# Gate stores of a streaming encoder layer issued from the sync queue instead of ScalarE's

## The chip, the cores and the metric

The kernel runs on one core of a Trainium2 chip. The metric is the device time of one execution in microseconds (us), as the median of several runs. Engines are named as in the profile: PE (matmul), PEld (its weight loads), DVE, ACT (ScalarE), POOL (GpSimd) and SP (the sync engine). SP computes nothing here; it issues transfers. "SPq" and "ACTq" are the instruction queues of SP and ACT where they issue transfers.

## The reference

One step of one encoder layer over 2048 prompt rows and 64 sample rows, 1024 channels, all in float32. Cut to what matters:

```python
h = rms_norm(x, norm1_g) * (1 + sc1) + sh1
z = h @ w_in
glu_a, glu_b, q, k, v, g_conv, g_attn = split(z)      # gates: 2 x 1024 columns
u = glu_a * sigmoid(glu_b)
conv_out = conv_module(u)        # causal depthwise conv of 31 taps, LayerNorm, swish, w_conv_out
o = attend(rms_norm(q), rms_norm(k), v)               # own chunk of 64 and the 8 before it
attn_out = o @ w_attn_out
merged = sigmoid(g_conv) * conv_out + sigmoid(g_attn) * attn_out
x = x + gt1 * (merged @ w_o)
h2 = rms_norm(x, norm2_g) * (1 + sc2) + sh2
x = x + gt2 * ((silu(gate) * up) @ w_ffn_out)         # gate, up = split(h2 @ w_ffn_in)
```

## The kernel before

Every float32 operand of a matmul is split into a high and a low part, and a product is three matmuls (high by high, high by low, low by high), so `hh`/`hl` are the two parts of the normalised input, `whi`/`wlo` those of a weight, `ph`/`pl` those of the softmax.

The 2112 rows are worked off in four blocks, `PBLOCKS`, of 576, 512, 512 and 512 rows. The first phase runs through `ORDER`: for each block the columns of `w_in` in eight stages, `q, 0, k, 1, v, 2, 3, g`. Numbered stages are the GLU pairs of the convolution, `g` the gates. Attention, convolution, norms of the next block and the splitting of weights are laid between the projection's matmuls as generators. Stage `g` of the four blocks lies at about 182 to 320, 481 to 612, 764 to 887 and 1029 to 1171 us. Then the mixers are merged over three column blocks, and the feed-forward part follows.

In stage `g` the inner function `part` of `gates` computes one tile of 128 gate columns by up to 512 rows: 24 matmuls into `ps`, a tanh on ACT from `ps` into a temporary tile `t` named "gate", and a store of that tile to the DRAM tensor `g_d`. There are 84 such tiles: 32 of 128x288 in the first block, 44 of 128x512 and 8 of 128x256 in the others. The merge reads `g_d` back much later (`gate_columns`, L1133).

The tile comes from `temp`:

```python
NT, NS = 7, 2
def temp(name, shape=(P, 512)):
    return wk.tile(list(shape), F32, tag="t", name=name, bufs=NT)
```

All temporaries with tag "t" share these seven buffers, among them `ln` (the convolution's norm), `other` (half of an attention output), `r`/`t` (roots of the norms) and the gates. A buffer is handed on when its last reader is done; for a gate the reader is the store.

What sets the order around the change: PE's order is that of the code, fixed by hand up to the end of the first phase. The orders of ACT, DVE, POOL and SP are laid by a scheduler from the dependences, so a transfer stands in its issuing engine's queue at one place among that engine's other instructions. Each engine works its queue in order; one that waits holds what is behind it. Besides the gates, SP's queue carries the loads of weights (L385 the raw ones, L480 the split ones read back, L515 the split ones written), of keys, queries and values (L1464, L1465, L1471, L1473), of the attention's bias (L1517), of the next block's input rows (`x_t` L1146, `x_c` L1159), and the stores of the attention and convolution parts (`o_d` L1495, `c_d` L1363). `x_t` is squared and summed on ACT; from the sums POOL makes the roots `r`, PE transposes them (`pt`), and the next block's norm goes on from there. All transfers, from either queue, share a set of eight completion semaphores in turn, and one that takes a semaphore waits for the landing of the transfer that had it before.

Of the kernel before, what the change touches and what calls it, by code (L numbers as in the profile page):

```python
# [73 lines left out]
def halves(lo, hi):  # L74
    n = hi - lo
    if n <= 512:
        return [(lo, hi)]
    mid = lo + n // 2
    return [(lo, mid), (mid, hi)]


def tile_chunks(lo, hi):

    tiles = token_tiles(lo, hi)
    t, n = tiles[(len(tiles) + 1) // 2 - 1]
    return [(lo, t + n), (t + n, hi)]
# [537 lines left out]
def streaming_layer(ctx: ExitStack, tc: tile.TileContext, I, O):  # L624
    nc = tc.nc
# [24 lines left out]
    g_d = dram.tile([2, KT, P, T], F32, name="g_d")  # L650
# [127 lines left out]
    def temp(name, shape=(P, 512)):  # L778
        return wk.tile(list(shape), F32, tag="t", name=name, bufs=NT)
# [467 lines left out]
    def columns(wh, wl, hh, hl, c0, c1):  # L1247

        nk = len(wh)
        ps = ps_g.tile([P, 512], F32, tag="gp", name="ps")  # L1250
        for k in range(nk):
            mm3(ps[:, : c1 - c0], wh[k], wl[k], hh[k][:, c0:c1], hl[k][:, c0:c1], k == 0, k == nk - 1)
        return ps

    def kts(t, a=0, b=KT):
        return [t[:, k] for k in range(a, b)]
# [132 lines left out]
    def gates(b, free):  # L1389

        o = PBLOCKS[b][0]
        w = PBLOCKS[b][1] - o

        def part(g, ws, c0, c1):
            ps = columns(*ws, kts(hh), kts(hl), c0, c1)
            t = temp("gate")
            stream.after("act", "pe")
            act.activation(t[:, : c1 - c0], ps[:, : c1 - c0], AF.Tanh, scale=0.5)
            nc.scalar.dma_start(g_d[g // 8, g % 8, :, o + c0 : o + c1], t[:, : c1 - c0])

        def pair(g):
            ws = [W.get(("in", 2560 + g * P, h)) for h in range(2)]
            return [[[w[l][:, k, e * P : e * P + P] for w in ws for k in range(4)] for l in range(2)] for e in range(2)]

        n = 16 - SPLIT_G if b + 1 < len(PBLOCKS) else 16
        for g in range(0, n, 2):
            for e, ws in enumerate(pair(g)):
                for c in halves(0, w):
                    part(g + e, ws, *c)
                if e:  # L1410
                    W.done()
                    W.done()
                yield g + e
        rest = [ws for g in range(n, 16, 2) for ws in pair(g)]
        for c0, c1 in ((0, w // 2), (w // 2, w)):
            for i, ws in enumerate(rest):
                part(n + i, ws, c0, c1)
                if c1 == w and i % 2:
                    W.done()
                    W.done()  # L1420
            free["columns"] = c1
# [531 lines left out]
    c0, c1 = tile_chunks(*CBLOCKS[0])  # L1953
# [517 lines left out]
```

## Time and profile before

| | us |
|---|---|
| runs | 2931.04, 2938.12, 2940.68 |
| median | 2938.12 |
| profiled execution | 2935.84 |
| its span | 2934.1 |
| PE busy in the span | 2877.2 |
| ACT busy | 1366.9 |

The times of a span are of one execution; the execution's own time is 1.74 us longer than the span. "Busy" of an engine leaves out the issuing of transfers. The granted TensorE clock was 0.993 of full speed on average. By the windows over stage `g` and what lies between, the engines were busy as follows (window, length, busy us of PE, PEld, DVE, ACT and POOL with counts, granted clock, busy share of the DMA engines, GB/s):

```profile
180.00:320.00 140.00, 128.80 (x921) 124.81 (x919) 99.31 (x204) 78.64 (x176) 25.90 (x23) 0.94 0.90 299
...
480.00:612.00 132.00, 127.20 (x715) 109.03 (x717) 94.78 (x186) 82.27 (x148) 13.36 (x12) 0.99 0.92 285
...
764.00:887.00 123.00, 121.75 (x687) 105.29 (x686) 87.91 (x177) 79.65 (x143) 12.25 (x12) 1.00 0.94 290
...
1029.00:1175.00 146.00, 142.78 (x790) 122.84 (x789) 104.05 (x201) 98.70 (x174) 23.33 (x15) 1.00 0.85 256
```

In a row of waits, the engine named first waits, "<-" names who ended the wait, and the numbers are total us, times, and the longest.

### The profile page before, as it was taken

The numbers are of one execution on the slowest core, as the hardware profiler recorded it, in microseconds if no ns is written. First come the engines' busy times: TensorE is split into PE (matmuls) and PEld (weight loads), VectorE is DVE, ScalarE is ACT, GpSimd is POOL, SyncE is SP. The second block draws the span as 40 slices with busy tenths as digits, with TensorE's granted clock in tenths as the row PEclk, the third lists the DMA queues.
The fourth block names the chain that finished last, engine by engine and source line by source line (L and its number), as shares of the span: only waits on it lengthen the run. The fifth ranks groups of instructions, "written<-read, shape, count | busy, mean of one in ns | idle before, by whom it ended". The sixth has DMA issues, their size and how long they took to land.

```text
span 2934.1 us, 44538 instructions
## 1 busy us (share of the span) xinstructions
PE 2877.2 (98%) x16130; PEld 2578.7 (88%) x16130; DVE 2044.7 (70%) x3621; ACT 1366.9 (47%) x2441; POOL 1170.4 (40%) x742
## 2 busy tenths in 40 slices
PE   8998999999999999999999999999999999999999
PEld 6798878788888888898999998999999999999998
DVE  5995688578867886487777756666666557566666
ACT  4345634661465267464434345444444345444442
POOL 1301310101011102454566452366667742465767
PEclk9998999999999999999999999999999999999999
DMA  8989889988997897884444876232333965333333
GB/s 320 331 299 320 278 284 307 288 282 288 292 309 233 298 272 238 287 311 166 147 144 144 290 253 215 94 125 87 115 123 104 344 223 180 97 101 108 115 107 127
DMA packets 313788, 634.28 MB, mean 216 GB/s; under 512 B 36864, under 2 KB 133664, under 8 KB 313568
## 3 DMA queue, kind: packets, MB, share of 16 engines
q1 hardware_dynamic: 300464, 612.88, 63.3%
q10 hardware_dynamic: 13104, 18.56, 1.8%
q8 instruction: 127, 2.08, 0.3%
q14 instruction: 93, 0.76, 0.1%
HBM read 482.81 MB, written 148.51 MB: 215 GB/s over the span
## 4 chain that ended last, share of the span: by engine, by line
PE 48%; DVE 2%; ACT 1%; issue 0%; POOL 0%; ACTq 0%; DVEq 0%
PE ps L106 29%; PE pd L106 14%; PE pw L106 5%; DVE wlo L106 1%; DVE pw L106 0%; ACT whi L106 0%; DVE ps L106 0%; DVE t L106 0%; DVE sums L106 0%; PE pt L106 0%; DVE acc L106 0%; ACT xn L106 0%; DVE hid L106 0%; ACT hid L106 0%; DVE b L106 0%
## 5 line engine op out<-in xcount | busy, mean ns | idle before, releaser
L106 PE MATMUL ps<-t,whi 128*128 128x384 f32 (+1 forms) x2112 | 502.1, 322 | 2.1 <-ACT u L106 0.8
L106 POOL TENSOR_TENSOR wlo<-wst,whi 128x1024 fp32r<-128x1024 f32 (+1 forms) x159 | 363.2, 2296 | 239.9 <-ACT whi L106 204.8
L106 ACT ACTIVATE whi<-wst 128x1024 fp32r<-128x1024 f32 (+1 forms) x265 | 257.9, 978 | 294.4 <-PE ps L106 126.7
L106 PE MATMUL ps<-b,whi 128*128 128x384 f32 (+1 forms) x1584 | 378.4, 324 | 4.8 <-DVE v L106 2.1
L106 PEld LDWEIGHTS ps<-t,whi 128*128 128x128 f32 x2112 | 367.6, 188 | 9.5 <-ACT u L106 3.0
L106 DVE SCALAR_TENSOR_TENSOR y<-u,wd,y 128x512 f32<-128x512 f32 (+1 forms) x480 | 369.3, 773 | 7.7
L106 PE MATMUL ps<-hh,whi 128*128 128x512 f32 (+2 forms) x992 | 364.2, 367 | 0.0
L106 DVE TENSOR_TENSOR acc<-acc,pd 128x512 f32<-128x512 f32 x482 | 322.3, 685 | 48.6 <-PE pd L106 46.1
L106 PE MATMUL ps<-hh,wlo 128*128 128x512 f32 (+2 forms) x992 | 346.3, 349 | 0.0
L106 PE MATMUL ps<-hl,whi 128*128 128x512 f32 (+2 forms) x992 | 345.9, 349 | 0.0
L106 PE MATMUL ps<-t,wlo 128*128 128x384 f32 (+1 forms) x1056 | 338.2, 321 | 0.0
L106 PE MATMUL pd<-whi,hid 128*128 128x512 f32 x912 | 297.3, 391 | 0.3 <-DVE hid L106 0.3
L106 PEld LDWEIGHTS ps<-b,whi 128*128 128x128 f32 x1584 | 275.6, 188 | 12.9 <-DVE v L106 3.2
L106 ACT ACTIVATE pr<-pr,sm 128x640 f32<-128x640 f32 (+3 forms) x272 | 202.5, 749 | 154.4 <-DVE sm L106 152.3
L106 PE MATMUL ps<-b,wlo 128*128 128x384 f32 (+1 forms) x792 | 255.0, 322 | 0.0
L106 POOL TENSOR_TENSOR r<-t,mhalf 128x8 f32<-128x8 f32 (+4 forms) x54 | 86.3, 1599 | 395.6 <-DVE t L106 385.4
L106 PEld LDWEIGHTS ps<-hh,wlo 128*128 128x128 f32 x992 | 188.0, 189 | 23.1
L106 PEld LDWEIGHTS ps<-hh,whi 128*128 128x128 f32 x992 | 188.6, 190 | 17.3 <-issue 2.5
L106 PEld LDWEIGHTS pd<-whi,hid 128*128 128x128 f32 x912 | 171.1, 188 | 36.3 <-ACT hid L106 0.7
L106 DVE TENSOR_TENSOR wlo<-wst,whi 128x1024 fp32r<-128x1024 f32 (+1 forms) x106 | 134.5, 1276 | 97.6 <-ACT whi L106 96.4
L106 PEld LDWEIGHTS ps<-hl,whi 128*128 128x128 f32 x992 | 188.9, 190 | 14.8 <-issue 1.7
L106 PEld LDWEIGHTS ps<-t,wlo 128*128 128x128 f32 x1056 | 198.1, 188 | 0.8
(235 smaller groups left out, 6274.6 us busy)
## 6 DMA issues: line engine op xcount, KB each, us to landing
whi<-w_din_h SPq DMA_DIRECT2D x72, 512.0 KB, 6.1
wlo<-w_din_l SPq DMA_DIRECT2D x72, 512.0 KB, 6.9
wst<-sum_d SPq DMA_DIRECT2D x131, 256.0 KB, 2.9
wfo<-in_w_ffn_out SPq DMA_DIRECT2D x64, 512.0 KB, 3.9
sum_d<-ws SPq DMA_DIRECT2D x88, 256.0 KB, 2.2
wst<-in_w_ffn_in SPq DMA_DIRECT2D x85, 256.0 KB, 2.9
wst<-in_w_ca SPq DMA_DIRECT2D x35, 512.0 KB, 5.2
wst<-in_w_ffn_in SPq DMA_DIRECT2D x35, 512.0 KB, 4.6
```

The lines of the kernel that those rows point to most:

```text
L106: self.last = f(*args, **kw)
```

## The change

The store of a gate tile is issued by `nc.sync` instead of `nc.scalar`; the code around it stays.

```diff
             t = temp("gate")
             stream.after("act", "pe")
             act.activation(t[:, : c1 - c0], ps[:, : c1 - c0], AF.Tanh, scale=0.5)
-            nc.scalar.dma_start(g_d[g // 8, g % 8, :, o + c0 : o + c1], t[:, : c1 - c0])
+            nc.sync.dma_start(g_d[g // 8, g % 8, :, o + c0 : o + c1], t[:, : c1 - c0])
```

The scheduler places the 84 stores in SP's queue, between its loads, and orders ACT's and DVE's work anew around them; PE's order in the first phase stays. Numbers behind a name tell instances apart.

SP in the first block's gates, where the fourth `x_t` of the next block is loaded, as it stands after the change (`part_l` is a half of an attention part, `kk` keys, `wst` a raw weight):

```order
L1495 DMA o_d_66<-part_l_2924 128x64
L1399 DMA g_d_68<-gate_2953 128x288
L1399 DMA g_d_68<-gate_3010 128x288
L385 DMA wst_3055<-in_w_qkv 128x1024
L515 DMA w_din_4096_1_h_3057<-whi_3017 128x1024
L515 DMA w_din_4096_1_l_3058<-wlo_3018 128x1024
L1517 DMA bias_192<-in_rel_bias 64x576 x2
L1464 DMA kk_1714<-q_d_63 64x2x64
L1465 DMA kk_1714<-k_d_64 64x320
L1464 DMA kk_1714<-q_d_63 64x2x64
L1465 DMA kk_1714<-k_d_64 64x320
L1399 DMA g_d_68<-gate_3079 128x288
```

The three rows of gates are new; all others stood in the same order before, and four rows further down follows the load of `x_t_3092`.

ACT at the same place, from the difference of the two orders (`ph` is half of a softmax, `whi` a weight's high part, `ssq` the sums of squares):

```order
 L106 ACTIVATE gate_3189<-ps_3140 128x288
 L106 ACTIVATE ph_3177<-ptp_3176 128x128
-L1399 DMA g_d_68<-gate_3189 128x288
+L106 ACTIVATE ln_3221<-y_774,lnh_176 128x64
+L106 ACTIVATE x_t_2892,ssq_2902<-x_t_2892 128x1024
 L106 ACTIVATE ph_3177<-ptp_3176 64x64
-L106 ACTIVATE ln_3221<-y_774,lnh_176 128x64
+L106 ACTIVATE x_t_2894,ssq_2902<-x_t_2894 128x1024
+L106 ACTIVATE x_t_2896,ssq_2902<-x_t_2896 128x1024
```

The store leaves ACT, and the squares of three `x_t`, which stood further up before, now follow the tanh of gate_3189.

SP in the last block's gates, from the difference (`cin` are the merge's first inputs, `tg` the gates read back):

```order
 L1471 DMA vv_11756<-v_d_65 128x8x128
+L1141 DMA cin_11850<-c_d_67 128x4x320
 L1141 DMA cin_11852<-c_d_67 128x4x320
 L1141 DMA cin_11851<-o_d_66 128x4x320
+L1399 DMA g_d_68<-gate_11843 128x512
 L1141 DMA cin_11853<-o_d_66 128x4x320
 L1133 DMA tg_11858<-g_d_68 128x320
```

One store comes in ahead of the last `cin` and of `tg`, and one `cin` has moved down to here; queries, keys and bias for the next group of heads follow behind `tg`.

## The prediction

> **What bounds the kernel now.** I read the page's busy times first, then PE's waits, then the two queues that issue transfers, then single stretches of the four gate stages. The page's first lines, the queue of ScalarE's transfers and the chain of waits:
>
> ```profile
> PE 2877.2 (98%) x16130; PEld 2578.7 (88%) x16130; DVE 2044.7 (70%) x3621; ACT 1366.9 (47%) x2441; POOL 1170.4 (40%) x742
> ...
> q10 hardware_dynamic: 13104, 18.56, 1.8%
> ...
> PE 48%; DVE 2%; ACT 1%; issue 0%; POOL 0%; ACTq 0%; DVEq 0%
> ```
>
> PE is busy for 2877.2 of 2934.1 us, so everything but PE together explains 56.9 us. ACT is at 47%, and ACTq, the queue that issues the 84 stores, has 0% of the chain. A change that only relieves ACT can gain next to nothing; what counts is PE's waits:
>
> ```profile
> PE sc L106 <- DVE sm L106: 9.5, 5, 4.0
> PE pt L106 <- DVE kn L106: 8.7, 4, 4.2
> PE pt L106 <- POOL r L106: 7.2, 1, 7.2
> PE sc L106 <- DMA kk<-k_d: 4.1, 3, 2.3
> ...
> PE ps L106 <- DMA wlo<-w_dqkv_l: 1.5, 2, 0.8
> ...
> PE ps L106 <- ACT gate L106: 1.4, 1, 1.4
> ```
>
> Columns are total us, times, longest. Only one short wait is for a gate's tanh, and the store follows the tanh, so nothing of that 1.4 us goes. The gates' own rows, and what the sync queue waits for:
>
> ```profile
> L106 ACT ACTIVATE gate<-ps x84: 364/576/602, 182.3 to 1170.1; 128x512 f32<-128x512 f32 x44, 128x288 f32<-128x288 f32 x32, 128x256 f32<-128x256 f32 x8
> L1399 ACTq DMA_DIRECT2D g_d<-gate x84: 326/326/359, 182.7 to 1170.8; - x84
> ...
> DMA to landing us min/median/max: 1.7/5.3/8.7
> ```
> ```profile
> SPq L1464 <- DMA g_d<-gate: 23.9, 8, 7.6
> ...
> SPq L1465 <- DMA g_d<-gate: 17.4, 6, 4.6
> ```
>
> Two things show here. A store costs its issuer 0.326 us and lands 5.3 us later. And SP already waits for stores that it did not issue: 23.9 + 17.4 us in 14 waits at two lines alone, since the transfers of both queues take their completion semaphores in turn.
>
> **The change part by part.** Removed: 84 issues of 0.326 us on ACT, 27.4 us. ACT has the other 53% of the span free, so I price it at 0; what covers it is PE's own work, and without that cover 27.4 us would be its limit. Added: the same 84 issues on SP, priced per issue by SP's rows below (0.38 to 0.61 us), 32 to 51 us of SP. PE never waits for SP itself, so this too counts only where a load that PE needs comes later. The bytes (18.56 MB) stay. The real cost is that SP is one queue in order: a store placed in it waits for its tanh, and every load behind it waits along. So I went through the 84 places in SP's new order and compared when SP issued the next load before with when the tanh ended.
>
> *Block 0 (180 to 320 us).* SP runs behind ACT here, so 31 of the 32 stores find their tanh done and cost an issue alone. The stretch holds the two longest stalls of all gate stages. Rows of SP's queue, ACT, DVE, POOL and PE (start, length, engine, what, and in brackets the idle time before it and who ended it):
>
> ```profile
> 253.88 0.61 SPq L1464 DMA_DIRECT2D q<-q_d  x1
> 259.10 0.46 SPq L1465 DMA_DIRECT2D kk<-k_d  x1
> ...
> 265.67 0.38 SPq L1495 DMA_DIRECT2D o_d<-part_l  x1
> ...
> 273.06 0.60 SPq L1465 DMA_DIRECT2D kk<-k_d  x1
> ...
> 276.19 0.50 SPq L1146 DMA_DIRECT2D x_t<-in_x_prompt  x1
> ```
> ```profile
> 266.58 0.41 ACT L106 ACTIVATE gate<-ps 128x288 f32<-128x288 f32 x1 [0.71 <-PE ps L106]
> ...
> 272.36 0.41 ACT L106 ACTIVATE gate<-ps 128x288 f32<-128x288 f32 x1
> ...
> 283.41 1.06 ACT L106 ACTIVATE x_t<-x_t 128x1024 f32<-128x1024 f32 x1 [5.05 <-DMA x_t<-in_x_prompt]
> ```
> ```profile
> 275.36 0.29 DVE L106 CUSTOM_DVE_ANT_0 pr<-sc,bias 128x128 f32<-128x128 f32 x1 [3.59 <-DMA bias<-in_rel_bias]
> ```
> ```profile
> 284.84 1.02 POOL L106 TENSOR_TENSOR r<-t,mhalf 128x4 f32<-128x4 f32 x1 [10.10 <-DMA c_d<-part_l]
> ```
> ```profile
> 268.09 0.19 PE L106 MATMUL po<-ph,vv 128*128 128x64 f32 x1
> ...
> 275.72 0.79 PE L106 MATMUL sc<-kk,q 128*128 128x256 f32 x2 [3.96 <-DVE sm L106]
> ...
> 285.92 0.48 PE L106 MATMUL pt<-ident,r 128*128 128x128 f32 x1 [7.24 <-POOL r L106]
> ```
>
> PE waits 3.96 us until 275.72, because the bias load came late, and 7.24 us until 285.92, because the fourth x_t, issued at 276.19, was there only at 283.41 (square, then r, then pt). Both loads are in SP's queue, so the change can move both stalls, and this is where the sign is decided.
> For earlier: the gap between 254.49 and 259.10 is a wait for a landed gate, 4.61 us, which leaves when SP carries the stores itself; and the stores of gate_3137, 3189 and 3247, which ACT had issued before x_t landed, now stand behind that load.
> For later: by the order 24 of the block's stores stand ahead of the fourth x_t, five of them after 249 us (gate_2832 to gate_3079), 5 x 0.4 = 2 us against the 4.61 us; the others went before it partly into SP's own waits. And the tile that a gate is written to comes from a ring of seven, shared with the norm and attention temporaries; it is free when its store has landed. By the order, gate_2953's store goes behind part_l at 265.67, so it is issued near 266.1 and lands near 271.3; gate_3189 takes that tile, and its tanh, at 266.58 before, comes 4.8 us later. Behind it on ACT stand ph, on which PE's po at 268.09 waits, and now also the x_t squares. PE's work between 268.09 and 271.76 (3.7 us) then runs until about 277, past the 275.72 at which bias let it go on: the first 3.96 us of lateness are covered by that wait. Likewise gate_3079's store goes behind kk at 273.06, lands near 279, and gate_3247's tanh, 272.36 before, waits 6.6 us for it; that falls into PE's wait for r. The fourth x_t is issued behind these, by my count between 276 and 279.
> Bounds: −11.2 us (both stalls gone, 3.96 + 7.24) and +10 (x_t 7 us later and 3 us of slower clock after it). I take +2, the middle of x_t's 0 to 3 us plus the uncovered half microsecond of po, because the issue times of SP are nearer to this case than a queue that runs ahead.
>
> The clock's price is in the windows around these stalls (columns: window, length, busy us of PE, PEld, DVE, ACT, POOL, granted clock, DMA share, GB/s):
>
> ```profile
> 270.00:280.00 10.00, 4.72 (x25) 4.13 (x23) 2.29 (x7) 3.99 (x9) 2.34 (x1) 0.70 0.98 318
> 280.00:290.00 10.00, 4.08 (x17) 4.07 (x18) 3.68 (x8) 1.88 (x5) 1.02 (x1) 0.50 1.03 354
> 290.00:300.00 10.00, 10.00 (x74) 9.91 (x73) 5.78 (x23) 5.43 (x13) 0.00 (x0) 0.95 0.82 305
> ```
>
> The clock granted falls to 0.50 behind the stalls and is 0.95 again after 290: a stall that vanishes would bring a little more than its length, one that appears cost a little more. The Trainium skill, "TensorE: Matmul & The Clock Gate", Part 1 (The HAM clock gate), says that the clock goes to half after at least one idle window of about 3.4 us; by that rule the 3 us that I put into block 3 below leave it at full and the sum as it is, 2940.2, and a wait just longer than the window would bring an estimated 1.7 us more (half of 3.4 us at half clock), 2942; the 0.70 and 0.50 behind waits of 3.96 and 7.24 us agree with it. The DMA engines are full there (0.98 and 1.03), so a store that stands behind loads gives its share to them.
>
> *Block 1 (481 to 612).* From the second store on, SP is ahead of the tanh and gets held. In the order x_t 2 and 3, issued at 517.77 before, go behind gate_6018, whose tanh ends at 553.17 + 0.60 = 553.77:
>
> ```profile
> 517.77 0.90 SPq L1146 DMA_DIRECT2D x_t<-in_x_prompt  x2
> ```
> ```profile
> 553.17 0.60 ACT L106 ACTIVATE gate<-ps 128x512 f32<-128x512 f32 x1
> ```
> ```profile
> 536.45 0.90 PE L106 MATMUL sc<-kk,q 128*128 128x320 f32 x3 [2.29 <-DMA kk<-k_d]
> ```
>
> With them 1 MB leaves the traffic ahead of the kk loads, for which PE waits at 536.45. Bounds: −4.1 us (all waits on kk gone) and +3 (three weights as late as the longest weight wait above, 0.8 us, and half a microsecond elsewhere). I take −1, a little under half of the longest such wait: the keys themselves are issued no earlier, only the traffic ahead of them thins. Behind the third and later stores SP is held 1 to 9 us by a tanh; the weights there are loaded further ahead than that, as PE's short waits on weights above let expect, so the +3 stays in the range alone.
>
> *Block 2 (764 to 887).* By the same comparison gate_8802 holds SP by 11 us and four others by 4 to 9 us; what covers it is again the distance at which keys and weights are loaded. Bounds −0.8 (the longest weight wait above gone) and +4 (five such holds at 0.8 us); I take +0.4, one issue ahead of a weight that came just in time.
>
> *Block 3 (1029 to 1171).* One place is uncovered. SP's loads here, the tanh of gate_11843 on ACT, the matmul that needs the keys, and the median landing of such a load:
>
> ```profile
> 1121.13 1.42 SPq L1133 DMA_DIRECT2D tg<-g_d  x2
> 1128.43 0.61 SPq L1464 DMA_DIRECT2D q<-q_d  x1
> ...
> 1130.39 0.63 SPq L1465 DMA_DIRECT2D kk<-k_d  x1
> ```
> ```profile
> 1128.74 0.58 ACT L106 ACTIVATE gate<-ps 128x512 f32<-128x512 f32 x1
> ```
> ```profile
> 1137.88 0.76 PE L106 MATMUL sc<-kk,q 128*128 128x320 f32 x4
> ```
> ```profile
> kk<-k_d SPq DMA_DIRECT2D x48, 256.0 KB, 7.6
> ```
>
> In the new order the store of gate_11843 stands ahead of the last cin load, tg and the keys. SP can issue it only at 1129.32; then one cin and two tg (about 2.1 us by their rows) and only then q, at 1131.8 instead of 1128.43: 3.4 us later, with the traffic of cin and tg now directly before it. The last kk, issued at 1130.39, is there by its median landing of 7.6 us at 1138.0, and PE takes it at 1137.88: nothing to spare. Bounds 0 (the shared engines make up for it) and +6 (the store's 5.3 us more); I take +3, the 3.4 us less some tenths in which the shared engines are not full.
>
> *The rest.* In the first merge, from 1190 us, PE's order differs in a few rows, and gates are read long after they landed: 0, within −1 and +1.
>
> Sum: 0 + 2 − 1 + 0.4 + 3 + 0 = +4.4 us. The profiled execution took 2935.84 us, 1.74 around its span of 2934.1: 2940.2. That execution lies 2.28 us under the median of 2938.12; I put the new median at 2941, between 2940.2 and 2942.5. What a measurement of this kernel can tell from no change is 0.3%, 8.8 us, and so +3 or +4 reads as the same.
>
> **The rivals.** *Slower:* the ring of seven decides. If gate_2953's store lands later than 271.3, by the 8.7 us that the slowest store took instead of 5.3, ACT and with it po, the squares and x_t all shift: 4.8 + 3.4 = 8.2 us against a cover of 3.96, leaving 4.2; with x_t as late (7 us) after it, and +3 in block 3, it is 2948 to 2952. It decides once the fourth x_t lands later than 290. For it speak 0.98 and 1.03 of DMA share; against it that ACT itself idles 5.05 us before x_t's square.
> *Faster:* SP stops waiting for landed gates (41.3 us at two lines), runs 4 to 7 us ahead, x_t and bias land before PE asks. Then 3.96, 7.24 and some 2.3 us on kk go, +3 stays: 2935.84 − 10.5 = about 2925, 2927 as a median. It needs x_t at 269 instead of 276.19; against it stand the 24 issues added ahead of it, and the completion semaphores that SP's transfers still take in turn.
> *Weights late:* the holds of 9 to 11 us behind a tanh in blocks 1 and 2 exceed the spare time in two or three places, 3 to 4 us each, +10 in all, 2950. Against it: PE waits for no weight there by more than 0.8 us now.
> That the change does not do what it says is excluded: its order shows 84 stores on SP and none on ACT.
>
> *Hidden anyway:* the stores share the DMA engines with the loads from either queue, so only the 84 issues change places, 27.4 us on ACT and 32 to 51 on SP, and neither is on PE's path: 2935.84, as a median 2938. For it speaks ACTq's 0% of the chain; against it the order, in which the tanhs come ahead of loads. The Trainium skill, "DMA: Bandwidth & Descriptors", section Issuing engines are not separate DMA queues, states this rule: transfers from several engines run on the same 16 DMA engines, and spreading them only saves issue time on the sequencer. The trace agrees as far as bytes go, by the 0.98 and 1.03; no run here yet shows the rest.
>
> **How the numbers follow.** Forecast (2936 to 2947 as its own range): 0.38. Hidden anyway: 0.20, also within 0.3%. Slower by the ring in block 0: 0.17. Weights late: 0.10. Faster by SP's freed waits: 0.15. So faster 0.15, same 0.58, slower 0.27. The range goes to 2928 on one side, into the faster case, and to 2954 on the other, into both slower ones; about 0.08 and 0.10 are left out.
>
> **What would show it.** ACT without any issue of line 1399; SP's rows for it 84 times at 0.33 to 0.6 us; SP's waits turned from landed gates to ACT's gate in blocks 1 to 3, and about 11 us of them at gate_8802. PE's wait for r at about 286 of 7 to 10 us, for kk at 536 shorter, and a new wait of some 3 us for sc near 1138. ACT's tanh of gate_3189 near 271 with a wait on a store's landing. Wrong it would be if x_t's fourth load is issued before 272 or lands after 290, or if PE waits for weights in blocks 1 and 2.

## The result and the profile after

| | median us | runs | ratio to before, 95% |
|---|---|---|---|
| before | 2931.98 | 7 (2930.45 to 2940.68) | |
| after | 2946.16 | 7 (2944.65 to 2954.21) | 1.0045 [1.0032, 1.0057] |
| after, once more in a later session | 2947.20 | 6 (2942.11 to 2954.22) | 1.0038 [1.0024, 1.0053] |

Each ratio here and below is to the kernel before, run beside it on the same chip (medians of 2934.66 to 2936.88 us in the later sessions). The change made the kernel slower by 0.45%, 13 us by this ratio. The profiled execution took 2946.04 us, its span is 2943.9, 9.8 us more than before. The page's first lines after the change:

```profile
PE 2879.9 (98%) x16130; PEld 2581.5 (88%) x16130; DVE 2040.7 (69%) x3621; ACT 1366.7 (46%) x2441; POOL 1167.6 (40%) x742
...
q1 hardware_dynamic: 312560, 630.19, 64.6%
...
q10 hardware_dynamic: 1008, 1.25, 0.1%
```

The stores' bytes, 17.3 of the 18.56 MB of queue q10, have moved to q1, and PE's busy time grew by 2.7 us only: the other 7.1 us of the longer span are time in which PE waits. The longest of PE's waits after the change but the first, which hardly differs (total us, times, longest):

```profile
PE sc L106 <- DMA kk<-k_d: 9.4, 4, 4.6
PE pt L106 <- POOL r L106: 9.3, 1, 9.3
PE sc L106 <- DVE sm L106: 9.0, 5, 3.9
```

Waits for keys went from 4.1 to 9.4 us. SP's list of waits shows the other side:

```profile
SPq L1399 <- ACT gate L106: 136.3, 39, 7.9
```

Before, SP waited at 14 places of two lines (41.3 us, and 110 us over all lines) for a gate's store to land. That is gone but for 0.8 us; instead it waits 136.3 us, at 39 of the 84 stores, for the tanh. To see where PE falls behind, read the same matmul in both timelines. The first rows are of the kernel after:

```profile
274.80 0.51 PE L106 MATMUL sc<-kk,q 128*128 128x256 f32 x2 [1.41 <-DVE sm L106]
285.80 0.47 PE L106 MATMUL pt<-ident,r 128*128 128x128 f32 x1 [9.31 <-POOL r L106]
...
534.29 0.82 PE L106 MATMUL sc<-kk,q 128*128 128x320 f32 x4 [1.01 <-DMA kk<-k_d]
...
557.14 0.86 PE L106 MATMUL sc<-kk,q 128*128 128x320 f32 x4 [0.71 <-DVE sm L106]
...
610.35 1.43 PE L106 MATMUL sc<-kk,q 128*128 128x320 f32 x4 [4.58 <-DMA kk<-k_d]
...
634.05 0.82 PE L106 MATMUL sc<-kk,q 128*128 128x320 f32 x4 [1.22 <-DMA kk<-k_d]
...
893.47 1.43 PE L106 MATMUL sc<-kk,q 128*128 128x320 f32 x4 [3.92 <-DVE sm L106]
...
1045.19 0.83 PE L106 MATMUL sc<-kk,q 128*128 128x320 f32 x4 [1.48 <-DVE sm L106]
...
1147.35 1.10 PE L106 MATMUL sc<-kk,q 128*128 128x320 f32 x4 [2.60 <-DMA kk<-k_d]
...
1181.26 0.56 PE L106 MATMUL ps<-cin,whi 128*128 128x320 f32 x2 [1.39 <-ACT gate L106]
```

And of the kernel before, the counterparts of the rows at 557, 634, 1045 and 1181 (those of 275, 286 and 536 stand in the prediction):

```profile
561.53 0.84 PE L106 MATMUL sc<-kk,q 128*128 128x320 f32 x4 [1.34 <-DVE sm L106]
...
630.82 0.82 PE L106 MATMUL sc<-kk,q 128*128 128x320 f32 x4 [0.66 <-DMA kk<-k_d]
...
1038.49 0.83 PE L106 MATMUL sc<-kk,q 128*128 128x320 f32 x4 [1.48 <-DVE sm L106]
...
1170.78 0.56 PE L106 MATMUL ps<-cin,whi 128*128 128x320 f32 x2 [1.39 <-ACT gate L106]
```

PE stands at −0.1 us at 286, −4.4 at 557, +3.2 at 634, +6.7 at 1045 and +10.5 at 1181. So block 0 cost nothing, block 1 first gained 4.3 us, and then three new waits came: 4.58 us for keys at 610, 3.92 us at 893, 2.60 us for keys at 1147. In the second run of the changed kernel the same rows come 1.3 to 4.8 us later, with waits of 4.75, 3.92 and 3.01 us at these places; so the three come again, and the smaller shifts between them are not to be read closely.

PE loses more than the waits. From 557 to 634 it falls back by 7.6 us, of which the waits explain 5.1 (4.58, and 1.22 instead of 0.66). The rest is in matmuls that run slower behind the wait; the granted clock there (third column from the end), first before, then after the change:

```profile
610.00:620.00 10.00, 10.00 (x82) 8.14 (x81) 8.90 (x25) 6.29 (x13) 0.00 (x0) 1.00 1.04 408
```
```profile
610.00:620.00 10.00, 9.65 (x64) 7.30 (x65) 6.93 (x19) 4.79 (x10) 0.00 (x0) 0.74 0.93 313
```

### The profile page after: what moved, and what is told of

Same layout as the page of the kernel before. It is cut to its first block, busy times and chain, and to the rows that moved or that the text cites. A ratio compares the mean times of both kernels' runs of the same rounds, so it can differ in the third digit from the quotient of the medians.

```text
span 2943.9 us, 44559 instructions
## 1 busy us (share of the span) xinstructions
PE 2879.9 (98%) x16130; PEld 2581.5 (88%) x16130; DVE 2040.7 (69%) x3621; ACT 1366.7 (46%) x2441; POOL 1167.6 (40%) x742
## 5 line engine op out<-in xcount | busy, mean ns | idle before, releaser
L106 DVE TENSOR_TENSOR wlo<-wst,whi 128x1024 fp32r<-128x1024 f32 (+1 forms) x106 | 136.3, 1291 | 98.7 <-ACT whi L106 97.7
```

Of the source, the lines that this page charges most:

```text
L106: self.last = f(*args, **kw)
```

## The experiments

**Queue or order?** The change did two things: it put stores in SP's queue, and the scheduler then laid ACT's and DVE's instructions in another order. Two kernels separate them. An addition to the program, `pin`, gives the scheduler edges that fix the issue order of named instructions, each behind the one before it, and add no wait:

```diff
     with tile.TileContext(nc) as tc:
         streaming_layer(tc, ins, outs)
+        pin(nc, tc)
```

*sp_old_order*: stores on SP, with ACT, DVE, POOL and PE in the order of the kernel before.

> All 84 stores on the sync queue as in the changed kernel, but the order of ACT's, DVE's, POOL's and PE's instructions is held to that of the kernel before; only SP's queue differs. Theory 1 (the new order that the scheduler gave ACT and DVE costs the most: part_h and softmax steps later, which hold SP's loads and PE): PE's waits of 4.58 us at 610 and 3.92 us at 893 go, the one of 2.60 us at 1147 stays; ratio to before 0.998 to 1.002, 2927 to 2937 us. Theory 2 (the queue itself: a load that stands behind a store waits for its tanh): the waits at 610 and 893 stay, ratio 1.004 to 1.006, 2943 to 2949 us.

*act_new_order*: stores on ACT, with ACT, DVE, POOL and PE in the order of the changed kernel.

> All 84 stores on ACT's queue as before, but ACT, DVE, POOL and PE in the order of the changed kernel. Theory 1: the waits near 610 and 893 appear although no store is on SP, and part of the gain in block 1 is gone: ratio 1.003 to 1.005, 2940 to 2946 us. Theory 2: as before, ratio 0.998 to 1.001, 2927 to 2935 us.

Measured: sp_old_order 2963.53 us, ratio 1.0088 [1.0071, 1.0104]; act_new_order 2937.78 us, 1.0004 [0.9993, 1.0015]. Theory 1 falls in its main point: the new order by itself costs nothing that can be told (by the interval at most 0.15%, 4.4 us), and without it the change would cost twice as much. Of the two waits that it foresaw in act_new_order, the one at 893 is there (3.92 us), the one at 610 is not. In sp_old_order, ACT's timeline and SP's rows show what the scheduler had evaded:

```profile
518.80 1.06 ACT L106 ACTIVATE x_t<-x_t 128x1024 f32<-128x1024 f32 x1 [13.81 <-DMA x_t<-in_x_prompt]
...
832.74 1.06 ACT L106 ACTIVATE x_t<-x_t 128x1024 f32<-128x1024 f32 x1 [17.73 <-DMA x_t<-in_x_prompt]
```
```profile
499.02 0.32 SPq L1399 DMA_DIRECT2D g_d<-gate  x1
...
509.60 2.36 SPq L1146 DMA_DIRECT2D x_t<-in_x_prompt  x3
```
```profile
PE ptp L106 <- ACT pr L106: 21.8, 2, 11.7
```

The load of x_t stands behind gate stores in SP's queue and is issued at 509.60 (494.72 in the kernel before). ACT, which has x_t's square at the old early place, stands 13.81 and 17.73 us for it, and PE waits 21.8 us for the softmax behind that square. In the changed kernel the squares are further back on ACT, and these two waits don't exist. The waits at 610 and 893 are gone, as theory 1 and not theory 2 expected; but ACT and DVE have their old order there and PE also comes 11 to 26 us later, and this run does not tell which of the two removed them.

**Which store?** The prediction named gate_11843's store as the one that holds the keys in the last block.

```diff
-            nc.sync.dma_start(g_d[...], t[...])
+            (nc.scalar if b == 3 and g == 10 else nc.sync).dma_start(g_d[...], t[...])   # one_back
+            (nc.scalar if b == 3 and g in (8, 9) else nc.sync).dma_start(g_d[...], t[...])   # keep_11721
```

> The changed kernel with one store of the 84, that of gate_11843 in the last block, back on ACT; all orders else as in the changed kernel. If that store holds the keys behind its tanh, PE's wait of 2.60 us at 1147 goes and the time falls by about 3.4 us against the changed kernel: ratio to before 1.0033, about 2943 us. If the keys are late for another reason (traffic of the cin and tg loads), the wait stays and the ratio is 1.0045, 2946 us.

one_back measured 2943.59 us, 1.0023 [1.0014, 1.0032]. The wait stayed, 2.79 us at 1148.56, so this store alone does not make it. (That the ratio is lower than the changed kernel's 1.0038 to 1.0045 is not explained by that place; the intervals touch, and the spans of the two profiles, 2943.6 and 2943.9, are nearly equal.) SP's rows of the changed kernel show an earlier hold:

```profile
1113.86 1.12 SPq L1517 DMA_DIRECT2D bias<-in_rel_bias  x2
1121.55 0.33 SPq L1399 DMA_DIRECT2D g_d<-gate  x1
1121.97 0.38 SPq L480 DMA_DIRECT2D whi<-w_din_h  x1
...
1136.04 0.34 SPq L1399 DMA_DIRECT2D g_d<-gate  x1
...
1138.04 0.61 SPq L1464 DMA_DIRECT2D q<-q_d  x1
```

SP stood from 1114.98 to 1121.55 for the tanh of gate_11721, with four weight loads, `cin` and the keys behind it; then all of them came at once. Gate_11843's store, held for its own tanh, went out at 1136.04, and the keys behind it.

> The changed kernel with two stores of the last block, of gate_11631 and gate_11721, back on ACT. With the store of gate_11843 back on ACT PE's wait of 2.60 us near 1147 stayed; SP's queue stood 6.6 us for the tanh of gate_11721, with four weight loads, cin and the keys behind it. If that hold makes the keys late, the wait goes under 1 us and the time falls by about 3 us. If it is the amount of traffic between 1121 and 1140, it stays.

keep_11721 puts two stores back, those of gates 9 (gate_11721) and 8 (gate_11631). It measured 2943.23 us, 1.0026 [1.0015, 1.0036], and its whole list of PE's waits between 1100 and 1170 us is one row:

```profile
PE sc L106 <- DMA kk<-k_d: 0.7, 1, 0.7
```

The wait went from 2.6 to 0.7 us, although gate_11843's store stands where it stood and is still held. So the earlier holds make the keys late, by the loads that they bunch in front of them; which of the two stores counts, and whether the hold of gate_11843 adds to it, is not separated. The 4 us against the second run of the changed kernel lie within the intervals.

**The wait at 610.** In the changed kernel, SP's rows there:

```profile
586.29 0.40 SPq L1495 DMA_DIRECT2D o_d<-part_l  x1
594.27 0.32 SPq L1363 DMA_DIRECT2D c_d<-part_h  x1
...
595.91 0.40 SPq L480 DMA_DIRECT2D whi<-w_dqkv_h  x1
```

SP stands 7.6 us for part_h, a store of the convolution that was in SP's queue before the change too, and that ACT does late in this order; the weights and the keys, issued from 598.46 on, are behind it. Yet the keys go out no later than in the kernel before. The last of them, and the time from issue to landing of those around it (last column), before and after:

```profile
602.97 0.60 SPq L1465 DMA_DIRECT2D kk<-k_d  x1
...
kk<-k_d SPq DMA_DIRECT2D x2, 256.0 KB, 5.0
```
```profile
601.06 0.44 SPq L1465 DMA_DIRECT2D kk<-k_d  x1
...
kk<-k_d SPq DMA_DIRECT2D x2, 256.0 KB, 9.2
```

They take longer to land, directly behind weights that went out 4 us later than before (595.91 against 591.54), and PE asks for them 4.2 us earlier, at 605.77 instead of 610.00. So in this place the wait takes back a lead: PE goes on at 610.35, 0.35 us later than before, and loses some 2.4 us more by the slower clock. In *weights_first* four weight loads go ahead:

```diff
 SP's queue near 590 us
-c_d<-part_h_6333, c_d<-part_l_6334, g_d<-gate_6439, whi_6446, wlo_6447, whi_6450, wlo_6451
+whi_6446, wlo_6447, whi_6450, wlo_6451, c_d<-part_h_6333, c_d<-part_l_6334, g_d<-gate_6439
```

> The changed kernel, with SP's queue alone altered at one place near 590 us: four weight loads go ahead of the stores of part_h_6333, part_l_6334 and gate_6439 instead of behind them. Theory Q (loads that stand in SP's queue behind a store that waits for ACT are the cost): PE's wait of 4.58 us at 610 goes to under 1.5 us and PE keeps its lead of some 4 us there, the time falls by 5 to 7 us against the changed kernel. Theory B (the keys are late because the DMA engines are full at that point whatever stands first): the wait stays at 4 to 5 us and so does the time.

Measured 2946.74 us, 1.0036 [1.0024, 1.0048], against 1.0038 of the changed kernel on the same chip, whose expectation was:

> The changed kernel once more, as the yardstick of the three others on the same chip: ratio to before 1.003 to 1.006 by every theory. The trace should show again PE's waits on kk near 610 (4 to 5 us), on sm near 893 (3.9) and on kk near 1147 (2.6).

The DMA engines' share of the same ten microseconds, 590 to 600, first of the changed kernel, then of weights_first (last three columns: clock, DMA share, GB/s), and PE's next wait in weights_first:

```profile
590.00:600.00 10.00, 10.00 (x82) 9.86 (x81) 6.96 (x17) 9.28 (x19) 0.00 (x0) 1.00 0.63 205
```
```profile
590.00:600.00 10.00, 10.00 (x78) 9.65 (x77) 7.51 (x20) 7.61 (x15) 0.00 (x0) 1.00 1.05 391
```
```profile
635.15 1.41 PE L106 MATMUL sc<-kk,q 128*128 128x320 f32 x4 [5.61 <-DMA kk<-k_d]
```

The hold had left the DMA engines idle for a third of the time, and taking it away filled them and took the wait at 610 down to 0.53 us (at 609.05; PE led by 1.9 us there, not by 4.4). But the time is the same: PE then waits 5.61 us at 635 instead of 1.22. Neither theory said so. Behind the mended place the next loads again stand behind a gate's store: SP waits 2.5 us for the last tanh of that block, issues its store at 612.02 and only then, at 612.43, the next weights, the modulation weights and keys. The last of these keys goes out at 622.22, as in the kernel before (622.18), but the keys take 12.5 us to land instead of 8.0 behind loads that started about 3 us later. With one hold removed, the next one counts.

**The wait at 893.** Here PE waits for DVE, whose order differs: the softmax step pr_9388 comes after the normalisation of x_c_9071, where it came first in the kernel before. *dve_pin* puts it back:

```diff
 DVE near 885 us
-pl_9404, pl_9429, pl_9448, x_c_9071 (9 steps), hl, hl, pr_9388
+pr_9388, pl_9404, pl_9429, pl_9448, x_c_9071 (5 steps), pr_9494, x_c_9071 (4 steps), hl
```

> The changed kernel, with DVE's order altered at one place near 885 us: the softmax step pr_9388 goes ahead of the normalisation of x_c_9071, as in the kernel before; SP's queue is that of the changed kernel. If the wait of 3.92 us at 893 comes from the order that the scheduler gave DVE, it goes to under 1 us and the time falls by 4 to 5 us. If the bias or the keys are late for pr_9388 anyway, the wait stays.

Measured 2942.85 us, 1.0028 [1.0018, 1.0039]. The wait is gone; PE's longest there is now the first row, and the second is the softmax step on DVE, put back to its old place:

```profile
895.76 0.50 PE L106 MATMUL ps<-whi,hh 128*128 128x512 f32 x1 [1.21 <-DMA whi<-w_dqkv_h]
```
```profile
884.40 0.82 DVE L106 CUSTOM_DVE_ANT_0 pr<-sc,bias 128x640 f32<-128x640 f32 x1 [2.26 <-DMA bias<-in_rel_bias]
```

So PE's wait for DVE does come from the order. But not all that PE loses here does: with the old order DVE stands 2.26 us for the attention's bias, PE 1.21 us for weights, and from 870 to 905 (times of the kernel before) PE falls back by 3.7 us, instead of 5.4 in the changed kernel. So loads are late here as well. The kernel with the stores on ACT and the new order has the wait too (3.92 us at 892.18). In its profiled execution it costs: the span is 4.4 us longer than before (2938.5 against 2934.1). Its median is the same as before within −2 and +4.4 us, so what the wait is worth at the end is not told. Whether dve_pin itself is faster than the changed kernel is open, since the intervals overlap.

**All stores later, or only some.** If every hold counts, the cure is to let no store reach the head of SP's queue before its tanh. *defer_6000* and *defer_12000* write the store down later in the program, by 6 or 12 us of planned time, and so the scheduler puts it further back:

```diff
-            nc.sync.dma_start(g_d[...], t[...])
+            stream.at(stream.when("act") + 12000.0, lambda: nc.sync.dma_start(g_d[...], t[...]))
```

> All 84 stores on the sync queue, each written down about 6 us of planned time (one gate) later than its tanh, so that the scheduler puts it behind loads that can go at once. Theory H (each store holds the loads behind it until its tanh ends; with one hold taken away at 590 us the wait of 4.58 us only moved from 610 to 635, to the next store): SP's waits for ACT's gates fall from 136 us to under 50, PE's waits at 610, 635 and 1147 go to under 1.5 us each, ratio to before 0.997 to 1.001, 2927 to 2938 us. Theory I (84 issues more on SP's queue cost the time, wherever they stand): ratio 1.003 to 1.005, 2944 to 2950 us.

> The same with about 12 us, two gates, of delay. A gate's tile stays taken longer out of the ring of seven. Theory H without a cost of the ring: as with 6 us or slightly better. If the ring matters, ACT waits for landings of gates before its tanhs and ln, 3 us and more in sum, and the time is at least 0.2% above that of the 6 us version.

*block0_only* has only the first block's 32 stores on SP, *three_fixed* joins the three local edits, *block0_defer* has the first block's stores on SP with 12 us of delay and the rest on ACT.

> Only the 32 stores of the first block, where the tanh is done before SP comes to the store, on the sync queue; the 52 others stay on ACT. Theory H: nothing is held there, ratio 0.998 to 1.001. Theory I: 32 of 84 issues, so about 0.38 of the loss, ratio 1.001 to 1.002, 2940 to 2943 us.

> The changed kernel with the three local edits together: four weight loads ahead of held stores near 590 us, DVE's softmax step ahead of x_c near 885, the stores of gate_11631 and gate_11721 back on ACT; 82 stores stay on the sync queue. If the losses at the three places add up to what the change costs and are not given back, the ratio to before is 0.999 to 1.001, 2932 to 2938 us. If PE's lead is lost again at the next load that stands behind a store, as from 610 to 635 when only the first place was mended, the ratio is 1.001 to 1.003, 2938 to 2944 us.

> A candidate better than both: the first block's 32 stores on the sync queue, written down 12 us of planned time after their tanh, which shortened PE's waits at 275 and 285 us by about 5 us in the version that did so for all blocks; the 52 later stores on ACT, where they hold no loads. If both effects stand, ratio 0.996 to 0.999, 2924 to 2932 us; if the gain at 285 is lost at the next late keys, 0.999 to 1.001.

| kernel | stores on SP | SP's wait for gates, us | median us | ratio to before, 95% | PE at 562, us | PE at 1171, us |
|---|---|---|---|---|---|---|
| after, second run | 84 | 135.8 | 2947.20 | 1.0038 [1.0024, 1.0053] | −1.8 | +13.6 |
| three_fixed | 82 | 127.1 | 2940.52 | 1.0015 [1.0003, 1.0028] | −3.0 | +5.5 |
| defer_6000 | 84 | 30.8 | 2942.19 | 1.0023 [1.0014, 1.0032] | −6.4 | +9.8 |
| defer_12000 | 84 | 10.4 | 2938.31 | 1.0008 [1.0000, 1.0017] | −11.5 | +2.4 |
| block0_only | 32 | 4.5 | 2936.24 | 1.0002 [0.9992, 1.0011] | −3.9 | −7.1 |
| block0_defer | 32 | none listed | 2932.69 | 0.9991 [0.9979, 1.0003] | +1.9 | +0.5 |

The third column is this row of SP's waits, of defer_6000, defer_12000 and block0_only in turn (it is of another line number where the store moved):

```profile
SPq L1401 <- ACT gate L106: 30.8, 9, 8.9
```
```profile
SPq L1401 <- ACT gate L106: 10.4, 3, 7.1
```
```profile
SPq L1399 <- ACT gate L106: 4.5, 6, 1.8
```

The last two columns say by how much PE starts a matmul later (+) or earlier (−) than the kernel before starts the same one, at 561.53 and at 1170.78 us. They come from one profiled execution each, which can lie some 7 us off its kernel's median.

The same 84 issues on SP cost 0.4% with 136 us of holds and 0.1% with 10 us, and both defer_12000 and block0_only came out below what theory I gave them (1.003 to 1.005, and 1.001 to 1.002, into which block0_only's interval just reaches): theory I (84 issues cost the time, wherever they stand) does not hold as it was put. But the sum of SP's waits for gates is not the price either. three_fixed has 127 us of them and defer_6000 31 us, and their times cannot be told apart. Between the two matmuls PE falls back by 15 us in both executions of the changed kernel, and still by 16 and 14 us in the two delayed ones. What makes defer_12000 shorter in these executions is the lead that it has at 562, and not a smaller loss behind it. With the three edits PE falls back by 8.5 us, and not at all where the later 52 stores are on ACT. So it is the stores of blocks 1 to 3 in SP's queue, with the order that the scheduler makes around them, that cost the time. How the loss is made where few gates hold SP is shown in part only: defer_12000 still has 4.63 us at 603 for keys, and there SP stands 9.5 us, from 577.60 to 587.20, for part_h:

```profile
SPq L1363 <- ACT part_h L106: 9.5, 1, 9.5
```

It reaches that place 7 us earlier than the changed kernel, and loses there a part of the lead that it had gained since 285:

```profile
282.38 0.32 PE L106 MATMUL pt<-ident,r 128*128 128x128 f32 x1 [3.14 <-POOL r L106]
...
603.33 1.41 PE L106 MATMUL sc<-kk,q 128*128 128x320 f32 x4 [4.63 <-DMA kk<-k_d]
```

I had expected the 6 us of delay to be enough and the waits at 610 and 1147 to go; neither was so, and its ratio of 1.0023 lies between the ranges of the two theories. The ring of seven tiles did not show: with 12 us of delay the time is lower, not 0.2% above. three_fixed came out as in its second expectation: PE waits 4.71 us at 632, for the next keys, as in weights_first. block0_defer, the candidate, is at 0.9991 with an interval that includes 1: not shown to be faster than the kernel before, and clearly faster than the changed one. Its trace does not have the gain in block 0 for which it was made: PE's wait for r is 6.9 us, and PE stands at +2.3 us at 286.

## Why the prediction was right or wrong

The range (2928 to 2954) held the time; the likeliest value, 2941, did not say enough: forecast were +4.4 us, measured 13 (1.0045), so it was the case to which I had given 0.27, slower, and not the 0.58 of no change that can be told.

- *ACT's issues at 0.* Right: ACT lost 84 issues of 0.326 us and nothing came of it.
- *SP's issues at 0.* Right: 32 of them alone cost nothing (1.0002), 84 with few holds cost at most 0.17% by the interval, though there a lead in the first blocks covers a loss in the later ones, so that the price of the 52 later issues alone is not shown.
- *Block 0, +2.* Measured −0.1 at 286 (+1.2 in the second run). The ring's lateness was mis-sized: gate_3189's tanh came at 267.90, not near 271, and its row in ACT's timeline of the kernel after names PE as what it waited for, not a landing. The fourth x_t was squared at 283.30, as before (283.41):

```profile
267.90 0.41 ACT L106 ACTIVATE gate<-ps 128x288 f32<-128x288 f32 x1 [2.13 <-PE ps L106]
...
283.30 1.06 ACT L106 ACTIVATE x_t<-x_t 128x1024 f32<-128x1024 f32 x1 [6.13 <-DMA x_t<-in_x_prompt]
```

- *Block 1, −1.* The thinner traffic ahead of the keys was right and larger (the wait of 2.29 us at 536 fell to 1.01, that of 1.17 at 513 is not in the timeline any more, and PE led by 4.4 us at 557). The step that failed is "the weights there are loaded further ahead than that": it priced the holds behind the third and later stores by weights alone, and left them in the range. PE did wait for no weight there, but the keys stand behind the weights. SP stood up to 7.4 us at a time, for tanhs and for part_h; the DMA share fell to 0.63, the loads then came in a bunch, the keys late among them, and PE's lead and 3 us more were gone at 634.
- *Block 2, +0.4.* Failed in kind: the scheduler's new order on DVE gave a wait of 3.92 us, and when that order was put back, bias and weights were late instead (2.26 and 1.21 us). I had read SP's new order place by place, and DVE's only as a number of changed rows.
- *Block 3, +3.* The wait came where it was put and with 2.60 us. The hold that I had priced was there too, but it does not make the wait by itself: without it the wait stayed, and without the holds of gate_11631 and gate_11721 it went. I had looked for the store next to the keys, and not for the hold that bunches what follows. That the size fits is luck in part.
- *The rivals.* "Weights late" had the mechanism, at +10 us: a few holds exceed what is in hand. It was keys more than weights. "Slower by the ring" and "faster by SP's freed waits" did not come: SP's 110 us of waits for landings did go, but 136 us for tanhs took their place.
- *The signs.* x_t's fourth load was issued at 275.58 and squared at 283.30, and PE waited for no weight in the gate stages of blocks 1 and 2: neither sign of being wrong came. SP's longest wait for a tanh was 7.9 us, not 11. PE's wait for r, 9.3 us, and the shorter wait at 536 were as said.
- *The clock.* By the rule that I cited of the Trainium skill ("TensorE: Matmul & The Clock Gate", Part 1) the wait in block 3 would leave the clock at full. Most traces do not agree: after 2.60 us it was 0.89 in the window from 1140 to 1150, and in one_back 0.83 in the ten microseconds after a wait of 2.79 us; in the second run a wait of 3.01 us left it at 1.00 from 1152 to 1162. So a wait of this length can lower the clock or not; what decides is not shown.

```profile
1140.00:1150.00 10.00, 7.40 (x37) 6.14 (x36) 5.72 (x11) 5.77 (x9) 3.34 (x2) 0.89 1.05 302
```

What stays open: how much each of the three places is worth at the end. Each edit removed its wait, but only their sum (1.0015 against 1.0038, intervals that overlap a little) and the delay of 12 us moved the time clearly. Open too is why PE still loses 14 us behind 562 when SP hardly waits for gates.

## What to carry to other kernels

A store that is issued from the queue of the loads is a wait for its producer, placed in front of every load behind it; the 32 stores here whose producer was nearly always done cost nothing that can be told. Price it by going through the queue for the places where the producer ends later than the next load used to go, and follow each such hold to the next operand that the bound engine needs, since the loads held come out in a bunch and the first one late may stand several entries further on. Where stores must share the loads' queue, write them down late enough that they are ready when the queue reaches them; here that cut the cost from 0.4% to 0.1%, and leaving the later stores on ACT removed it. The sum of the holds does not give the price. And read the order that the scheduler made of the other engines too, because it can hide a large part of the cost (here half) or add a wait of its own.

## What the runs showed of the hardware

With the DMA engines busy for 0.88 of the time from 180 to 1175 us, a lead of 2 to 11 us that PE had won was given back, in whole or in large part, where the next keys came late: at 610 in the changed kernel, at 609 and 603 in the two with delayed stores, at 635 in weights_first. I had expected such gains to add up. The share alone does not do it: in block0_only, at 0.89, PE's lead of 3.9 us at 562 was still there at the matmul of 630.82 (4.6).

Behind a wait of 4.58 us the granted clock was 0.74 in the window from 610 to 620, and PE lost some 2.4 us more than it had waited.
